# Eight columns of an input projection: high and low weights side by side in one stationary tile

## The chip, the cores and the metric

The kernel runs on one core of one Trainium2 chip. The metric is the device time of one execution in microseconds (us), as the median of several runs. A profile shows one execution of the same program, with every instruction of the five engines: TensorE (PE, with its weight loads as PEld), VectorE (DVE), ScalarE (ACT), GpSimd (POOL) and SyncE (SP), whose queue issues nearly all DMAs here. Each engine takes its instructions in the order in which the program has them. An instruction that waits holds up all that stand behind it on its engine.

## The reference

One layer of a hybrid decoder (2048 tokens, width 1024): one input projection feeds four gated DeltaNet heads and four HGRN2 heads, then an output projection, an MLP and a gated embedding follow. Cut to what the change touches:

```python
proj = jnp.einsum('btd,dc->btc', hn, w_in[i]).astype(f32)
...
a_gdn = proj[..., OFF_GDN_A:OFF_GDN_B]      # 4 columns
b_gdn = proj[..., OFF_GDN_B:OFF_HG_F]       # 4 columns
...
beta = jax.nn.sigmoid(b_gdn)
g_dec = -jnp.exp(gdn_a_log[i].astype(f32)) * jax.nn.softplus(a_gdn + gdn_dt_bias[i].astype(f32))
o_a = gated_delta_rule_chunked(q_a, k_a, v_a, g_dec, beta)
```

`a_gdn` gives each DeltaNet head its decay, `b_gdn` its gate. These eight columns of the input projection are what the change is about.

## The kernel before

**Precision.** All large products are made to nearly float32 accuracy out of a faster format (`F32R`). A float32 operand is split into a high part (a rounded copy, made by ScalarE) and a low part (what is left, a subtraction on VectorE); `split` at L164 and L165 does this. A product then takes three passes over the stationary operand: high weights by high data, high weights by low data, low weights by high data.

**Tiling of the mixer stage.** The 2048 tokens go in four quarters `q` of 512. For each quarter 33 *works* are run one after another on TensorE. The first is `ab`: the eight columns, spread in a stationary tile of 128 columns so that the four decays come out on partitions 0 to 3 of the result and the four gates on partitions 32 to 35; the other columns are zero. Then come eight works for each of four heads, of 128 columns each: k, q, v and z of the DeltaNet head, then f, i, q and g of the HGRN2 head. A work is 8 blocks of 128 input rows by 3 passes, 24 matmuls of 128x128 by 128x512, all into one bank of PSUM (`mm_...`, L1072). This document counts the four `ab` works as blocks 0 to 3, by their quarter.

**Weights.** In the first quarter the weights of a work are loaded raw and split (`stage`, L484), and both halves are written to a cache in device memory (`keep`, L180). In the later quarters they are loaded back already split (`reload`, L185), one MB a work. Three such tiles exist at a time.

**The order around the works.** TensorE's and SyncE's orders are written by hand. Each work is cut into three *steps* of eight matmuls. After each step, and once in its middle, the clock of the kernel moves and the generators due then issue their next portion: their matmuls are put between those of the works. The DeltaNet mixers (`gdn_mixer`), the HGRN2 mixers (`hgrn_mixer`) and the decays' own post-processing (`decays`) are such generators, with their due steps in tables (`A_STEPS`, `B_STEPS`). VectorE's, ScalarE's and GpSimd's orders are chosen by a scheduler when the program is built, so an edit at one place can move other instructions on these engines.

**What runs at an `ab` block.** At blocks 1 to 3 the heads of the quarter before are still under way:

- head 2's DeltaNet recurrence, a chain from chunk to chunk: `psa` on PE (L764), `r` on DVE (L766), `psb` on PE (L769), `w` on ACT (L771), `psc` on PE (L774), the new state `S` on DVE (L776), and `psa` of the next chunk. Two of its chunks lie around the block.
- head 3's triangular solve on DVE (`pr`, `xs`: L698, L701, L703), whose result goes through device memory (`xd`, L708; `xt`, L715), is transposed on DVE (`xn`, L717) and used on PE (`psp`, L722). The next head's solve starts with copies into `pr` and `xs` (L693, L695).
- the HGRN2 heads: `qk_h`, `att_h` and `keys_h` (L820 to L860), and the closing norms of finished heads (`og`, `osq`, `hl`, `m`; `nrm` on PE, L270 and L271).
- the next quarter's data: scaling and splitting of `xt` on DVE and ACT.

**The decays.** `decays` takes the result of the block from PSUM. ScalarE adds the bias to the four decay rows (`sp`, L498) and takes the tanh of the four gate rows (`gb`, L500). Softplus follows as |sp| on DVE (`se`, L502), Exp and Ln on ACT (L503, L504, each with a load of ScalarE's tables), then two operations on DVE (L505, L506) and four running sums (L508). The sums go to device memory (`gd`, L512) and, transposed by PE (`ps_gb`, L519), into `gcol` (L522).

```python
            S.activation(sp, ps[0:4, :], AF.Identity, bias=dec[:, 1:2])
            V.memset(gb, 0.0)
            S.activation(gb[32:36, :], ps[32:36, :], AF.Tanh, scale=0.5)
```

## Time and profile before

| what | value |
|---|---|
| median of 3 runs | 2715.93 us (2712.65 to 2716.56) |
| span of the profiled execution | 2719.9 us |
| mean granted TensorE clock | 0.995 |
| matmuls on PE | 12745, of them 96 in the four `ab` blocks |
| start of the four `ab` blocks | 40.2, 285.5, about 544.1 and 805.4 us |
| mixer stage | about 40 to 1065 us |

The profile's page gives the busy time of each engine over the whole span; a timeline lists instructions in order of time, neighbours of one line merged. A row of the timeline has the start in us, the duration in us, the engine, the line and operation, what is written and read, the number of instructions merged, and in brackets, where the engine stood idle before it, for how long and what ended the wait. Durations of neighbours overlap a little: the next instruction starts before the last has written its end. A table by windows gives, for stretches of time, the busy time of each engine with the number of its instructions, the granted clock, the busy share of the DMA engines and the GB/s that they moved.

### The profile page before, as it was taken

What the parts mean: (1) busy time and instruction counts of PE and PEld (TensorE: products, weight loads), DVE (VectorE), ACT (ScalarE), POOL (GpSimd) and SP (SyncE); (2) the same over time, 40 slices, a digit from 0 to 9 for tenths busy, and PEclk for the clock granted to TensorE, in tenths of its full rate; (3) what the DMA queues carried; (4) which work ended last, traced back from release to release, by engine and by line L of the source; (5) the groups of instructions that cost most, each with busy time, mean ns of one, the idle gap of its engine ahead of it and who ended that gap; (6) DMA issues with size and microseconds to landing.
All of it is one profiled execution on the core that took longest, in us unless ns stands there. A gap on an engine that the chain in (4) does not pass through costs nothing.

```text
span 2719.9 us, 38475 instructions
## 1 busy us (share of the span) xinstructions
PE 2660.8 (98%) x12745; PEld 2215.1 (81%) x12745; DVE 2040.8 (75%) x4219; ACT 1464.0 (54%) x2940; POOL 118.5 (4%) x133
## 2 busy tenths in 40 slices
PE   8999999999999999998999999999999999999999
PEld 6788888888888887876788888888888888888887
DVE  7778878787777777576989867768787765567776
ACT  7665555465445455575655646555555545465432
POOL 0000000000000000011000000001000000001000
PEclk9999999999999999998999999999999999999999
DMA  8777777667666665887566457667454346577663
GB/s 282 273 237 255 236 263 242 216 214 241 213 201 221 223 213 164 271 281 231 177 232 228 175 178 240 216 202 244 164 196 163 139 172 207 193 256 247 216 212 131
DMA packets 268742, 589.24 MB, mean 217 GB/s; under 512 B 55658, under 2 KB 60232, under 8 KB 249344
## 3 DMA queue, kind: packets, MB, share of 16 engines
q1 hardware_dynamic: 266240, 582.59, 63.9%
q0 software_dynamic: 2304, 4.20, 0.9%
q8 instruction: 101, 1.65, 0.3%
q14 instruction: 97, 0.79, 0.1%
HBM read 419.75 MB, written 166.92 MB: 216 GB/s over the span
## 4 chain that ended last, share of the span: by engine, by line
PE 51%; DMA 3%; DVE 3%; issue 3%; ACT 1%; POOL 1%; SPq 0%; POOLq 0%; DVEq 0%; ACTq 0%
PE d L1143 22%; PE u L1143 22%; PE mmg L1143 6%; PE mmo L1143 1%; DMA raw_out<-in_w_out_dram 1%; DMA yo<-in_xT_dram 0%; PE mme L191 0%; POOL acc_y L234 0%; DMA b<-h1d 0%; DMA w_out<-cache_out 0%; DMA db<-hid 0%; DVE t L165 0%; DMA h1d<-yo 0%; POOL yo L1229 0%; DVE pr_g L698 0%
## 5 line engine op out<-in xcount | busy, mean ns | idle before, releaser
L1072 PE MATMUL mm<-xt,w 128*128 128x512 f32 x3072 | 784.1, 400 | 1.4 <-ACT zt_zg L577 1.1
L1072 PEld LDWEIGHTS mm<-xt,w 128*128 128x128 f32 x3072 | 553.3, 189 | 102.3 <-ACT zt_zg L577 1.5
L1143 PE MATMUL d<-db,da 128*128 128x512 f32 x2688 | 611.0, 389 | 0.5 <-ACT db L217 0.2
L1143 PE MATMUL u<-t,wu 128*128 128x512 f32 x2604 | 591.1, 389 | 0.0
L1143 PEld LDWEIGHTS d<-db,da 128*128 128x128 f32 x2688 | 504.3, 188 | 106.4 <-DVE db L218 1.0
L1143 PEld LDWEIGHTS u<-t,wu 128*128 128x128 f32 x2604 | 488.7, 188 | 101.5
L218 DVE TENSOR_TENSOR db<-db 128x512 fp32r<-128x512 f32 x224 | 159.9, 714 | 72.4 <-ACT db L217 71.7
L1495 DVE TENSOR_TENSOR u<-u,u 128x512 f32<-128x512 f32 x224 | 150.2, 681 | 58.1 <-PE u L1143 56.6
L1143 PE MATMUL mmo<-mixT,w_out 128*128 128x512 f32 x720 | 173.4, 402 | 11.8 <-DMA w_out<-cache_out 5.5
L217 ACT ACTIVATE db<-db 128x512 fp32r<-128x512 f32 x224 | 140.9, 629 | 78.2 <-DMA db<-hid 71.9
L1143 PEld LDWEIGHTS mmo<-mixT,w_out 128*128 128x128 f32 x720 | 139.5, 195 | 44.6 <-DMA w_out<-cache_out 5.9
L1143 PE MATMUL mmg<-h2T,wg 128*128 128x512 f32 (+1 forms) x792 | 174.8, 383 | 0.0
L1538 ACT ACTIVATE u<-u 128x512 f32<-128x512 f32 x128 | 80.8, 631 | 166.3 <-DVE u L1495 166.0
L1143 PEld LDWEIGHTS mmg<-h2T,wg 128*128 128x128 f32 x792 | 145.5, 188 | 29.1
L165 DVE TENSOR_TENSOR da<-da 128x512 fp32r<-128x512 f32 x128 | 93.7, 732 | 77.7 <-ACT da L164 77.1
L164 ACT ACTIVATE da<-da 128x512 fp32r<-128x512 f32 x128 | 80.5, 629 | 124.8 <-DMA da<-sumd 91.6
L164 ACT ACTIVATE wu<-a 128x512 fp32r<-128x512 f32 x124 | 75.0, 623 | 44.3 <-DMA a<-in_w_up_dram 43.0
L698 DVE TENSOR_TENSOR pr_g<-xs_g,sys_g 128x16 f32<-128x16 f32 (+14 forms) x240 | 94.4, 393 | 5.6
L165 DVE TENSOR_TENSOR wu<-a,wu 128x512 fp32r<-128x512 f32 x124 | 85.6, 693 | 10.8 <-ACT wu L164 10.5
L234 POOL TENSOR_TENSOR acc_y<-acc_y,sq_y 128x512 f32<-128x512 f32 x28 | 38.5, 1374 | 1261.6 <-ACT sq_y L233 1260.8
L1539 ACT ACTIVATE u<-u 128x512 f32<-128x512 f32 x128 | 80.5, 629 | 3.1
L165 DVE TENSOR_TENSOR da<-dr,da 128x512 fp32r<-128x512 f32 x96 | 66.3, 691 | 19.0 <-ACT da L164 16.5
(385 smaller groups left out, 3792.6 us busy)
## 6 DMA issues: line engine op xcount, KB each, us to landing
w<-cache_in SPq DMA_DIRECT2D x96, 1024.0 KB
db<-hid SPq DMA_DIRECT2D x224, 256.0 KB
cache_in<-w SPq DMA_DIRECT2D x32, 1024.0 KB
hid<-u SPq DMA_DIRECT2D x128, 256.0 KB
da<-sumd SPq DMA_DIRECT2D x128, 256.0 KB
a<-in_w_up_dram SPq DMA_DIRECT2D x124, 256.0 KB
hid<-ht SPq DMA_DIRECT2D x96, 256.0 KB
dr<-in_w_down_dram SPq DMA_DIRECT2D x96, 256.0 KB
```

What stands on the lines that cost most here:

```text
L164: S.activation(t[:, 0], raw, AF.Copy)
L165: eng.tensor_tensor(t[:, 1], raw, t[:, 0], ALU.subtract)
L217: S.activation(t[:, 0], plain(t), AF.Copy)
L218: V.tensor_tensor(t[:, 1], plain(t), t[:, 0], ALU.subtract)
L234: eng.tensor_tensor(acc, acc, sq, ALU.add)
L698: V.tensor_tensor(pr[:, :, :, 0:i], xs[:, None, :, 0:i].broadcast_to([P, 2, GC, i]), sys[:, 0:i, i : i + 2].rearrange("p j two -> p two j" ...
L1072: PE.matmul(ps, *terms[i], start=i == 0, stop=i == nt - 1)
L1143: PE.matmul(ps, a, b, start=start, stop=stop)
L1495: V.tensor_tensor(c[new], c[old], ps, ALU.add)
L1538: S.activation(c[k], c[k], AF.Relu)
L1539: S.activation(c[k], c[k], AF.Square)
```

## The change

For the `ab` work alone, the high weights of the eight columns are put into columns 0 to 63 of the stationary tile and the low weights into columns 64 to 127. One pass then makes the products of both with the same data. Per block of input rows two passes remain (all weights by high data, all weights by low data), 16 matmuls a work in place of 24; the low-by-low product comes with it. High and low results stand on partitions 0 to 35 and 64 to 99 of the bank and are added afterwards: ScalarE copies the lower 36 rows to SBUF, VectorE adds the upper 36 rows from PSUM, and what read PSUM before reads this sum.

- The raw load takes half the columns (128x8x64, rows of 256 bytes), the split works on half, the cache and its three reloads hold 512 KB in place of 1024 KB.
- The three steps of the work have 5, 5 and 6 matmuls in place of 8 each, and the generators' portions lie at the same steps.

```diff
+        def stage_ab():
+
+            raw = wp.tile([P, KD, P // 2], F32, tag="raw", name="raw_ab0", bufs=2)
+            nc.sync.dma_start(raw, w_ab[:, :, : P // 2])
+
+            def ready():
+                w = wp.tile([P, KD, P], F32R, tag="whl", name="w_ab0")
+                S.activation(w[:, :, : P // 2], raw, AF.Copy)
+                V.tensor_tensor(w[:, :, P // 2 :], raw, w[:, :, : P // 2], ALU.subtract)
+                return w
...
         def decays(ps, q):
 
             gb = mt(f"gb_{q}", "gb", 1, (36, QT))
-            sp = m2.tile([4, QT], F32, tag="tmp", name=f"sp_{q}")
+            rest = m2.tile([36, QT], F32, tag="th", name=f"ab_rest_{q}")
+            ab = m2.tile([36, QT], F32, tag="tmp", name=f"ab_{q}")
             se = m2.tile([4, QT], F32, tag="th", name=f"se_{q}")
-            S.activation(sp, ps[0:4, :], AF.Identity, bias=dec[:, 1:2])
+            S.activation(rest, ps[P // 2 : P // 2 + 36, :], AF.Copy)
+            V.tensor_tensor(ab, ps[:36, :], rest, ALU.add)
+            sp = ab[0:4, :]
+            S.activation(sp, sp, AF.Identity, bias=dec[:, 1:2])
             V.memset(gb, 0.0)
-            S.activation(gb[32:36, :], ps[32:36, :], AF.Tanh, scale=0.5)
+            S.activation(gb[32:36, :], ab[32:36, :], AF.Tanh, scale=0.5)
...
                 for k, xk in enumerate(xt):
+                    if h is None:
+                        terms += [(w[:, k, :], xk[:, 0, :]), (w[:, k, :], xk[:, 1, :])]
+                        continue
                     terms += [(w[:, 0, k, :], xk[:, 0, :]), (w[:, 0, k, :], xk[:, 1, :]), (w[:, 1, k, :], xk[:, 0, :])]
```

`keep_ab` and `reload_ab` do for this tile what `keep` and `reload` do for the others. In the built programs PE and SP have the same order as before but for the changed instructions. On VectorE and ScalarE the scheduler has moved others around blocks 0 to 3. For blocks 2 and 3 the order on VectorE after the chunk's state `S` is:

```
before: ... xs_g, r_g, xs_g, se, gb, pr_g, xs_g copy, m_h, sp, att_h, sp, att_h, scans x4, qk_h, xn_g, copy_predicated, S_g, og_g, osq_g, gbb
after:  ... r_g, xs_g, add(ab), xs_g, gg_h, pr_g, xs_g, se, xs_g, gb, pr_g copy, att_h, att_h, qk_h, sp, m_h, copy_predicated, sp, S_g, scans x4, og_g, osq_g, xn_g, gbb
```

(`sp` stands for the two operations of L505 and L506, which after the change work on the tile `ab`.) In block 1 `xn_g` stands behind the scans too, ahead of `og_g`, and `m_h` stands between the two `att_h`. On ScalarE the order before is bias, tanh, table load, Exp, `w_g`, table load, Ln; after the change it is copy, bias, tanh, `w_g`, table load, Exp, table load, Ln.

More of the change, by code (lines that the diff above doesn't have):

```diff
@@ L491, in stage, with keep_ab, reload_ab @@
             return ready
+        def stage_ab():
[6 more added lines that the diff above has]
+                return w
+            return ready
+        def keep_ab(w):
+            cached["ab"] = dr.tile([P, KD * P], F32, name="cache_ab")
+            nc.sync.dma_start(cached["ab"], w.bitcast(F32).rearrange("p k n -> p (k n)"))
+        def reload_ab(q):
+            w = wp.tile([P, KD, P], F32R, tag="whl", name=f"w_ab{q}")
+            nc.sync.dma_start(w.bitcast(F32).rearrange("p k n -> p (k n)"), cached["ab"])
+            return w
         def decays(ps, q):
             gb = mt(f"gb_{q}", "gb", 1, (36, QT))
-            sp = m2.tile([4, QT], F32, tag="tmp", name=f"sp_{q}")
+            rest = m2.tile([36, QT], F32, tag="th", name=f"ab_rest_{q}")
+            ab = m2.tile([36, QT], F32, tag="tmp", name=f"ab_{q}")
             se = m2.tile([4, QT], F32, tag="th", name=f"se_{q}")
-            S.activation(sp, ps[0:4, :], AF.Identity, bias=dec[:, 1:2])
+            S.activation(rest, ps[P // 2 : P // 2 + 36, :], AF.Copy)
+            V.tensor_tensor(ab, ps[:36, :], rest, ALU.add)
+            sp = ab[0:4, :]
+            S.activation(sp, sp, AF.Identity, bias=dec[:, 1:2])
             V.memset(gb, 0.0)
-            S.activation(gb[32:36, :], ps[32:36, :], AF.Tanh, scale=0.5)
+            S.activation(gb[32:36, :], ab[32:36, :], AF.Tanh, scale=0.5)
             V.tensor_scalar(gb[32:36, :], gb[32:36, :], 0.5, 0.5, ALU.mult, ALU.add)
@@ L971, in stage_work @@
             if j < len(works) and works[j][3] == 0:
-                staged[j] = stage(works[j][0], works[j][2])
+                staged[j] = stage_ab() if works[j][4] is None else stage(works[j][0], works[j][2])
         def split_work(j):
             if j < len(works):
-                split_w[j] = staged.pop(j)() if j in staged else reload(works[j][1], works[j][0])
+                if j in staged:
+                    split_w[j] = staged.pop(j)()
+                elif works[j][4] is None:
+                    split_w[j] = reload_ab(works[j][3])
+                else:
+                    split_w[j] = reload(works[j][1], works[j][0])
         def keep_work(j):
             if works[j][3] == 0:
-                keep(works[j][1], split_w[j])
+                if works[j][4] is None:
+                    keep_ab(split_w[j])
+                else:
+                    keep(works[j][1], split_w[j])
         def load_x(q):
```

## The prediction

> **What bounds the kernel now.** I read the page first, then tables by windows around the `ab` blocks, then the timelines there. The page has PE busy for 98% of the span, and the window from 560 to 820 us (one quarter, with its `ab` block) says it again, at full clock.

> ```profile
> 560.00:820.00 260.00, 253.97 (x1393) 215.20 (x1391) 198.21 (x580) 136.80 (x362) 13.83 (x17) 1.00 0.68 222
> 541.00:548.00 7.00, 7.00 (x39) 5.94 (x38) 7.00 (x19) 4.14 (x9) 0.00 (x0) 1.00 0.63 238
> 548.00:555.00 7.00, 6.52 (x32) 5.10 (x32) 6.89 (x22) 2.88 (x4) 0.00 (x0) 1.00 0.04 17
> ```

> The columns are the window, its length, the busy us of PE, PEld, DVE, ACT and POOL, then clock, DMA share and GB/s. The last two rows lie on block 2. Over the quarter VectorE has a quarter of its time free; here it has none: 7.00 of 7.00 us, then 6.89. So at the place of the change two engines bind, and the question is which of them a shorter block leaves as the bound.

> The timeline of block 2, and under it the same place of block 3:

> ```profile
> 551.12 0.36 DVE L776 SCALAR_TENSOR_TENSOR S_g<-S_g,cd_g,psc_g 128x128 f32<-128x128 f32 x1
> ...
> 551.54 0.49 PE L764 MATMUL psa_g<-S_g,y_kg 128*128 128x128 f32 x2 [0.48 <-DVE S_g L776]
> ...
> 812.89 0.49 PE L764 MATMUL psa_g<-S_g,y_kg 128*128 128x128 f32 x2 [0.46 <-DVE S_g L776]
> ```

> PE is through with the block at 551.06 and waits 0.48 us for `S_g`, which DVE only reaches at 551.12, in a queue without a gap. `psc_g`, which `S_g` needs, stands in PE's order ahead of the block's last 12 matmuls, so `S_g` is late for DVE's queue, not for its input. In block 1 PE and `S_g` arrive together, with no wait.

> **What is removed: 32 matmuls.** Block 0 runs its 24 without a gap:

> ```profile
> 40.22 5.73 PE L1072 MATMUL mm_ab<-xt,w_ab 128*128 128x512 f32 x24 [0.21 <-ACT sq_e L233]
> ```

> 5.73 / 24 = 0.24 us each, a little less without the last one's own end; I take 0.23. Eight fewer a block are 1.85 us, four blocks 7.4 us.

> **Where this goes, blocks 1 to 3.** PE comes to `psa_g` 1.85 us earlier. On DVE nothing up to `S_g` is changed or moved, and none of it waits for the `ab` matmuls, so `S_g` ends where it did and `psa_g` starts where it did. The wait grows from 0.48 to about 2.3 us (block 3 the same, block 1 from nothing to 1.9). Gain 0 in each. If DVE did come earlier by the whole 1.85 us, it would be 5.6 us over the three; I take 0, since the queue shows no gap.

> **What is added, and who is late.** A copy of 36x512 on ACT and an addition of 36x512 on DVE with one operand in PSUM, both at the head of the decays' chain. The rows of the chain in block 2, first ACT's, then DVE's, then the row of PE that waits for them:

> ```profile
> 550.98 0.43 ACT L826 ACTIVATE hb_h<-qk_h 128x256 f32<-128x256 f32 x1 [3.60 <-DVE qk_h L824]
> 551.31 0.67 ACT L498 ACTIVATE sp<-mm_ab,dec 4x512 f32<-4x512 f32 x1
> 552.00 0.59 ACT L500 ACTIVATE gb<-mm_ab 4x512 f32<-4x512 f32 x1
> 552.61 1.28 ACT L503 ACT_TABLE_LOAD   x1
> 555.24 0.63 ACT L503 ACTIVATE se<-se 4x512 f32<-4x512 f32 x1 [1.35 <-DVE se L502]
> 555.90 0.37 ACT L771 ACTIVATE w_g<-psb_g,cc_g 128x128 f32<-128x128 f32 x1
> 556.28 1.28 ACT L504 ACT_TABLE_LOAD   x1
> 557.58 0.63 ACT L504 ACTIVATE se<-se 4x512 f32<-4x512 f32 x1
> ```

> ```profile
> 558.24 0.68 DVE L505 SCALAR_TENSOR_TENSOR sp<-sp,se 4x512 f32<-4x512 f32 x1 [1.32 <-ACT se L504]
> 558.85 0.41 DVE L842 TENSOR_TENSOR att_h<-at_h_d,cst 128x256 f32<-128x256 f32 x1
> 559.19 0.47 DVE L506 TENSOR_SCALAR sp<-sp,nexpa 4x512 f32<-4x512 f32 x1
> 559.58 0.40 DVE L844 TENSOR_TENSOR att_h<-at_h,cst 128x256 f32<-128x256 f32 x1
> 559.91 1.35 DVE L508 TENSOR_TENSOR_SCAN gb<-one,sp 4x128 f32<-4x128 f32 x4
> 561.19 0.39 DVE L855 TENSOR_TENSOR qk_h<-qk_h,gg_h 128x256 f32<-128x256 f32 x1
> 561.51 0.42 DVE L717 STREAM_TRANSPOSE xn_g<-xt_g 128x256 f32<-128x256 f32 x1
> 561.87 0.68 DVE L860 COPY_PREDICATED att_h<-cst,at_h 128x256 f32<-128x256 uint32 x1
> 562.37 0.29 DVE L776 SCALAR_TENSOR_TENSOR S_g<-S_g,cd_g,psc_g 128x128 f32<-128x128 f32 x1
> 562.60 0.66 DVE L585 TENSOR_TENSOR og_g<-pso_g,zt_zg 128x512 f32<-128x512 f32 x1
> 563.20 0.66 DVE L587 TENSOR_TENSOR osq_g<-osq_g,q_g 128x512 f32<-128x512 f32 x1
> ```

> ```profile
> 561.99 0.71 PE L722 MATMUL psp_g<-xn_g,um 128*128 128x128 f32 x4 [0.38 <-DVE xn_g L717]
> ```

> DVE itself stands idle here, 1.32 us at 558.24, for the Ln. So the chain to the Ln sets DVE's time, and DVE's `xn_g` sets PE's at `psp_g`.

> The two new operations have no row of their own. The nearest are `gb` for the copy (512 columns from PSUM, 0.59) and `og_g` for the addition (512 columns, one operand in PSUM, 0.66). Rows of 4 and of 128 partitions take alike (L505 0.68, L585 0.66), so the 36 partitions do not matter. Bounds 0.5 to 0.8 each; I take 0.59 and 0.66. With the new orders:

> - ACT, copy: `hb_h` ahead of it is held by DVE until 550.98, so it starts at 551.31, where `sp` did, and ends at 551.9.
> - DVE, addition: it stands behind `r_g` and one reduction, so that its turn comes at about 552.9 (by the distances of starts around there); to 553.6.
> - ACT: bias to 554.3, tanh to 554.9, `w_g` (now ahead of the loads) to 555.3, table load to 556.6, Exp to 557.2, table load to 558.5, Ln to 559.15. Before, it ended at 558.21: 0.94 later. `w_g` comes earlier than it did, so `psc_g` on PE does not wait.
> - DVE from the Ln on, by the distance of starts (a little under the durations): `sp` 0.6, `m_h` 0.1, the predicated copy 0.5, the second `sp` 0.4, `S_g` 0.25, the scans 1.28, then `og_g` and `osq_g` 0.6 each, which now stand ahead of `xn_g`. The two `att_h` and `qk_h` have gone into the idle time before. 559.2 + 4.3 = 563.5, and `xn_g` ends at 563.95 where it ended at 561.93.

> So `psp_g` starts 2.0 us later. About 0.2 of it comes back at PE's next wait for DVE (`nrm_g`, quoted below for block 1), for `hl_g` is then early. Blocks 2 and 3, which have the same orders: +1.8 us each.

> Block 1 has a bigger wait at `psp_g` already:

> ```profile
> 299.85 0.17 DVE L695 COPY xs_g<-cst 128x8 f32<-128x8 f32 x1 [3.85 <-DMA xd_g<-xs_g]
> ...
> 301.30 0.15 DVE L280 TENSOR_SCALAR m_h<-m_h 128x4 f32<-128x4 f32 x1
> ...
> 303.91 0.71 PE L722 MATMUL psp_g<-xn_g,um 128*128 128x128 f32 x4 [1.35 <-DVE xn_g L717]
> ...
> 307.29 0.50 PE L271 MATMUL nrm_g<-hl_g,ones 128*128 128x512 f32 x1 [0.17 <-DVE hl_g L165]
> ```

> DVE is held until 299.85 by a transfer, and this covers the longer chain: by the same steps the Ln ends at 300.5, when DVE is at `att_h`. But `m_h` now stands between the two `att_h`, and its own transfer lands by 301.3 at the latest; I take 301.1. Behind it `att_h` 0.35, `qk_h` 0.33, `sp`, the copy, `sp`, `S_g` and the scans as above make 3.7, to 304.9, and `xn_g` ends at 305.35 instead of 303.86: +1.5, less 0.2 at `nrm_g`, is +1.3 us.

> **Block 0.** PE can end 1.85 us sooner, but the third work of the quarter needs the PSUM bank that DVE's convolution of the first work reads until 58 us:

> ```profile
> 46.07 1.06 ACT L164 ACTIVATE w<-raw 128x1024 fp32r<-128x1024 f32 x1 [1.90 <-DMA raw<-in_w_in_dram]
> ...
> 58.09 2.09 PE L1072 MATMUL mm<-xt,w 128*128 128x512 f32 x8 [0.35 <-DVE acc_kg L542]
> ```

> ACT waits until 46.07 for a transfer, and copy and addition lie under that wait; the rest of the chain starts where it did. I take 0, between -1.85 (the convolution moves up too) and +1.3 (copy and addition both count).

> The halves saved in the cache and in the first split bring nothing: in no row does PE or DVE wait for `w_ab` at blocks 1 to 3. [...]

> **Sum.** 0 + 1.3 + 1.8 + 1.8 = +4.9 us on the profiled 2719.9, 0.18%. The profile is 0.15% above the median, so the step carries over as it is, if the stages behind the mixers follow PE, as I assume: 2715.93 + 4.9 = 2720.8 us.

> **Rivals.**

> - *PE is the bound, and the whole 7.4 us comes off:* 2708.5 us. For it speaks PE's 98%; against it DVE's 7.00 of 7.00 us and the 0.48 and 0.46 us that PE already waits at the block's end. It needs slack in DVE that the rows do not have. 0.12. [...] The rows have a second full engine here.
> - *The saving dies at `S_g`, but the longer chain is hidden:* 2715.9, give or take 2.5. The 1.32 us that DVE idles before the Ln, and other matmuls that DVE holds up behind, would have to take it up. 0.23.
> - *Slower by more:* in the work after next PE waits for ACT's `y_qg`:

> ```profile
> 582.28 0.49 PE L659 MATMUL kk_g<-y_qg,y_kg 128*128 128x128 f32 x2 [1.05 <-ACT y_qg L551]
> ```

>   In the changed order a table load ahead of it stands behind a read of PE's `t_kg`. If ACT's whole load of 1.28 us comes on top in each of three quarters, it is 2720.8 + 3.8 = 2724.6. It decides if ACT has no slack left there. 0.25.
> - *My forecast:* 2720.8, its own range 2717.5 to 2723. 0.40.

> **Chances.** A measurement of this kernel can tell about 0.2%, 5.4 us, from no change: faster is below 2710.5, slower above 2721.4. The first rival and a tail of the second make faster 0.14. The third and 0.17 of my own case lie above: 0.42. The rest, 0.44, is within. The range, 2712 to 2725.5, takes in the second and third and leaves out the first.

> **What would show it.** Right: `psa_g` waits about 2 us for `S_g` at blocks 1 to 3; `psp_g` waits some 2.4 us for `xn_g` in blocks 2 and 3; the distance from `S_g` to the end of the Ln grows by about 1 us; PE's busy time falls by about 7 us and the span does not follow. Wrong: `S_g` comes earlier after the block's start than it did (the first rival), or `xn_g` is as early as before (the second), or `kk_g` waits over 2 us for `y_qg` (the third).

## The result, and the profile after

| | before | after |
|---|---|---|
| median of 8 runs each, side by side | 2716.18 us (2711.54 to 2719.97) | 2724.45 us (2719.33 to 2730.66) |
| ratio to before, 95% interval | 1 | 1.0037 (1.0026 to 1.0047) |
| span of the profiled execution | 2719.9 us | 2724.6 us |
| PE busy, matmul instructions | 2660.8 us, 12745 | 2653.8 us, 12713 |

The change makes the kernel slower: by 8.3 us between the medians, 10 us by the ratio (7 to 13 by its interval). The forecast was +4.9 us, and the likeliest of its three outcomes was no change clear of noise (0.44), ahead of slower (0.42). The time lies inside its range, near the upper end, but only because the range takes in the third rival, whose cause did not come (see below).

The three windows that opened the prediction, in the profile after (window, length, busy us of PE, PEld, DVE, ACT and POOL, granted clock, DMA share, GB/s):

```profile
560.00:820.00 260.00, 252.38 (x1373) 215.13 (x1372) 198.82 (x582) 135.15 (x361) 14.75 (x17) 0.99 0.66 221
541.00:548.00 7.00, 6.91 (x36) 5.55 (x36) 7.00 (x20) 4.80 (x10) 0.00 (x0) 1.00 0.44 164
548.00:555.00 7.00, 5.09 (x22) 3.91 (x22) 6.99 (x21) 1.76 (x3) 0.00 (x0) 0.88 0.13 54
```

DVE is as full as it was (6.99 of 7.00 us), and PE is busy for 1.4 us less in the last window. New is the last row's clock: 0.88 where it was 1.00. The timeline of block 2 after, PE's rows and those that they wait for:

```profile
551.77 0.34 DVE L803 SCALAR_TENSOR_TENSOR S_g<-S_g,cd_g,psc_g 128x128 f32<-128x128 f32 x1
...
552.16 0.49 PE L791 MATMUL psa_g<-S_g,y_kg 128*128 128x128 f32 x2 [1.91 <-DVE S_g L803]
...
552.40 4.58 PE L1110 MATMUL mm<-xt,w 128*128 128x512 f32 x12
...
560.87 0.63 ACT L531 ACTIVATE se<-se 4x512 f32<-4x512 f32 x1
561.53 0.68 DVE L532 SCALAR_TENSOR_TENSOR ab<-ab,se 4x512 f32<-4x512 f32 x1 [1.27 <-ACT se L531]
...
565.82 0.42 DVE L744 STREAM_TRANSPOSE xn_g<-xt_g 128x256 f32<-128x256 f32 x1
...
566.30 0.71 PE L749 MATMUL psp_g<-xn_g,um 128*128 128x128 f32 x4 [2.51 <-DVE xn_g L744]
...
567.49 3.40 PE L1110 MATMUL mm<-xt,w 128*128 128x512 f32 x8
...
586.33 0.38 PE L685 MATMUL kk_g<-y_kg 128*128 128x128 f32 x2
587.71 0.49 PE L686 MATMUL kk_g<-y_qg,y_kg 128*128 128x128 f32 x2 [0.99 <-ACT y_qg L578]
```

Both forecast waits are there: 1.91 us for `S_g`, 2.51 us for `xn_g`. And `psa_g` starts where it did: 7.44 us behind the start of its block (552.16 - 544.72), before 7.49 (551.54 - 544.05). But the 12 matmuls behind the first wait take 4.58 us, and the 8 behind the second 3.40 us. The same two groups before, and the start of `kk_g`, which is used below:

```profile
551.78 2.98 PE L1072 MATMUL mm<-xt,w 128*128 128x512 f32 x12
...
562.90 2.09 PE L1072 MATMUL mm<-xt,w 128*128 128x512 f32 x8
...
580.85 0.38 PE L658 MATMUL kk_g<-y_kg 128*128 128x128 f32 x2
```

After the change again, the same stretch in windows of 3.4 us, laid on the places where the trace's clock records change:

```profile
546.50:549.90 3.40, 3.40 (x20) 2.88 (x18) 3.40 (x10) 0.59 (x1) 0.00 (x0) 1.00 0.68 285
549.90:553.30 3.40, 1.49 (x8) 1.01 (x7) 3.40 (x12) 1.03 (x2) 0.00 (x0) 0.99 0.00 0
553.30:556.70 3.40, 3.40 (x10) 2.63 (x9) 3.32 (x11) 1.35 (x2) 0.00 (x0) 0.50 0.00 0
556.70:560.10 3.40, 3.40 (x22) 3.00 (x21) 1.17 (x4) 2.81 (x4) 0.00 (x0) 1.00 0.18 34
560.10:563.50 3.40, 3.40 (x20) 2.82 (x18) 2.13 (x7) 2.79 (x6) 1.01 (x1) 1.00 0.83 294
563.50:566.90 3.40, 0.89 (x7) 0.60 (x6) 3.40 (x9) 0.63 (x1) 0.00 (x0) 1.00 0.09 25
566.90:570.30 3.40, 3.40 (x12) 2.82 (x12) 3.17 (x8) 1.28 (x5) 0.00 (x0) 0.50 0.54 142
```

Read PE's busy time (the third number) against the clock of the row below. In the two windows that hold a wait PE is busy for 1.49 and 0.89 us of 3.4; in the window after each the granted clock is 0.50, and then it is whole again. In the profile before, no window between 40 and 1065 us is at half clock. After the change there are five: at 75.4 us (behind block 0), 553.3, 566.9, 816.1 and 829.7.

What this does to PE in block 2, from the first matmul of the block to the first `kk_g`, before and after:

```profile
544.05:580.85 36.80, 35.79 (x190) 29.55 (x188) 31.55 (x85) 22.82 (x58) 3.00 (x4) 1.00 0.62 197
544.72:586.33 41.61, 37.09 (x181) 30.45 (x180) 32.57 (x88) 23.54 (x59) 2.60 (x4) 0.92 0.51 175
```

PE stands idle for 4.5 us where it was 1.0: the 3.5 us more are the two waits, as forecast. But its busy time, which eight matmuls fewer should have brought down by about 1.85 us, went up by 1.3 us. The difference, an estimated 3.15 us, is near the 3.4 us that two windows at half clock can cost at most.

So there were two theories to tell apart. **A:** TensorE's waits lower its clock, and each half-clock window costs up to 1.7 us (half of 3.41 us, the length of one half-clock record in the trace) on top of the wait. **B:** the longer chain of the decays delays enough on ScalarE and VectorE to cost all of it, and the clock only goes along.

### The profile page after: what moved, and what is told of

It is laid out like the page before. It is cut to its first block, busy times and chain, and to the rows that moved or that the text cites. A ratio compares the mean times of both kernels' runs of the same rounds, so it can differ in the third digit from the quotient of the medians.

```text
span 2724.6 us, 38415 instructions
## 1 busy us (share of the span) xinstructions
PE 2653.8 (97%) x12713; PEld 2211.2 (81%) x12713; DVE 2040.6 (75%) x4223; ACT 1465.6 (54%) x2944; POOL 119.5 (4%) x133
## 4 chain that ended last, share of the span: by engine, by line
PE 53%; DMA 4%; DVE 4%; issue 3%; ACT 1%; POOL 1%; SPq 0%; POOLq 0%; DVEq 0%; ACTq 0%
PE u L1181 22%; PE d L1181 21%; PE mmg L1181 6%; PE mm L1110 2%; PE mmo L1181 1%; DMA raw_out<-in_w_out_dram 1%; POOL acc_y L234 1%; DMA yo<-in_xT_dram 0%; DMA b<-h1d 0%; DVE pr_g L725 0%; DMA rd_g<-m_g 0%; DMA w_out<-cache_out 0%; DVE t L165 0%; ACT sq_y L233 0%; PE mme L191 0%
## 5 line engine op out<-in xcount | busy, mean ns | idle before, releaser
L165 DVE TENSOR_TENSOR da<-da 128x512 fp32r<-128x512 f32 x128 | 95.9, 749 | 76.8 <-ACT da L164 76.0
L164 ACT ACTIVATE da<-da 128x512 fp32r<-128x512 f32 x128 | 80.5, 629 | 122.2 <-DMA da<-sumd 99.9
L164 ACT ACTIVATE wu<-a 128x512 fp32r<-128x512 f32 x124 | 75.1, 623 | 47.1 <-DMA a<-in_w_up_dram 45.4
L234 POOL TENSOR_TENSOR acc_y<-acc_y,sq_y 128x512 f32<-128x512 f32 x28 | 38.6, 1380 | 1260.0 <-ACT sq_y L233 1260.0
L165 DVE TENSOR_TENSOR wu<-a,wu 128x512 fp32r<-128x512 f32 x124 | 85.6, 692 | 9.5 <-ACT wu L164 9.0
L165 DVE TENSOR_TENSOR da<-dr,da 128x512 fp32r<-128x512 f32 x96 | 66.3, 690 | 17.3 <-ACT da L164 15.6
```

The lines of the kernel that those rows point to most:

```text
L164: S.activation(t[:, 0], raw, AF.Copy)
L165: eng.tensor_tensor(t[:, 1], raw, t[:, 0], ALU.subtract)
L234: eng.tensor_tensor(acc, acc, sq, ALU.add)
```

## The experiments

One measure serves them all: the stretch from the first matmul of an `ab` block to the first `kk_g` behind it (L658 before, L685 after). In block 2 it is 36.8 us before (580.85 - 544.05) and 41.6 us after (586.33 - 544.72). The spans of single profiles are too coarse for this: two of the kernel before are 2719.9 and 2711.2 us, while their stretches agree within 0.5 us a block. In the table "half clock" lists the starts of the half-clock windows between 40 and 1065 us, and the ratio is to the kernel before in runs on the same chip.

| kernel | blocks 0, 1, 2, 3 (us) | half clock at (us) | ratio (95%) |
|---|---|---|---|
| before | 28.2, 37.3, 36.8, 36.8 | none | 1 |
| before_again | 27.8, 37.7, 36.8, 37.0 | none | one run |
| after | 28.5, 37.9, 41.6, 41.6 | 75, 553, 567, 816, 830 | 1.0037 (1.0026 to 1.0047) |
| after_again | 28.6, 38.0, 40.0, 40.2 | 77, 565, 825 | one run, +6.9 us |
| e1_short_alone | 27.8, 35.8, 38.6, 37.6 | 548 | 0.9996 (0.9986 to 1.0006) |
| e2_long_chain_alone | 29.5, 38.7, 39.5, 39.2 | none | 1.0023 (1.0014 to 1.0032) |
| e3_fill_waits | 27.4, 38.8, 38.9, 38.9 | 75 | 1.0016 (1.0007 to 1.0025) |
| e5_fill_half | 27.3, 38.4, 38.6, 38.4 | 75 | one run, +6.0 us |
| w1_wait_in_before | 27.8, 41.2, 39.7, 38.2 | 306, 566 | one run, +8.7 us |
| e4_defer_softplus | 28.3, 36.7, 39.4, 39.5 | 563, 822 | 1.0021 (1.0013 to 1.0030) |
| p1_hgrn_on_pool | 28.6, 41.3, 41.3, 39.8 | 289 (two windows), 572, 814 | 1.0039 (1.0026 to 1.0051) |
| p2_decays_on_pool | 31.7, 40.3, 43.5, 44.0 | 60, 309, 569 (two), 821, 835 (two) | 1.0061 (1.0047 to 1.0075) |
| p3_both_on_pool_after | 31.9, 44.1, 41.7, 43.2 | 59, 288 (two), 571, 814, 834 | 1.0062 (1.0049 to 1.0074) |
| p3_both_on_pool_before | 30.2, 43.3, 41.3, 41.6 | 290, 311, 553, 833 | 1.0046 (1.0033 to 1.0058) |
| v1_later_after | 28.1, 40.6, 37.0, 38.6 | 76, 308 (two windows), 827 | 1.0004 (0.9995 to 1.0014) |
| v1_later_before | 28.3, 37.6, 37.8, 38.7 | 812 | 1.0010 (1.0002 to 1.0019) |
| v4_later_half | 28.5, 38.5, 39.2, 39.2 | 566, 826 | 1.0010 (1.0001 to 1.0020) |
| v3_later_nrm_after | 28.3, 37.3, 38.4, 36.8 | 76, 568 | 0.9992 (0.9983 to 1.0001) |
| v3_later_nrm_before | 28.4, 37.3, 38.8, 37.2 | 559 | 1.0007 (0.9997 to 1.0016) |
| v5_later_and_defer | 28.6, 36.8, 35.8, 35.6 | none | 0.9976 (0.9966 to 0.9986) |

### The two parts of the change, each alone

`e1_short_alone`: the 16 matmuls with the packed tile, the decays as they were.

```diff
...
-            S.activation(rest, ps[P // 2 : P // 2 + 36, :], AF.Copy)
-            V.tensor_tensor(ab, ps[:36, :], rest, ALU.add)
-            sp = ab[0:4, :]
-            S.activation(sp, sp, AF.Identity, bias=dec[:, 1:2])
+            S.activation(sp, ps[0:4, :], AF.Identity, bias=dec[:, 1:2])
...
```

> Two theories of the 8.3 us that the changed kernel lost (2724.45 against 2716.18). Theory A, the clock: the waits of psa for S_g (1.9 us) and of psp for xn (2.5 us) in blocks 2 and 3 each let TensorE's granted clock fall to half for one 3.4 us stretch, some 1.7 us lost each time, on top of the waits themselves. Theory B, the chain alone: the copy and the addition make the decays late on ScalarE and VectorE, and this costs all of it. Here the block keeps its 16 matmuls, but the decays read rows 0 to 36 of mm_ab directly, with no copy and no addition (the products of the low weights are computed and left out of the result). A: psa still waits about 1.9 us for S_g, so one half-clock stretch stays after it in blocks 2 and 3, psp waits no more than before (about 0.4 to 1 us): 2717 to 2720. B: nothing is late but S_g, whose time does not depend on the change, so the time is that of before or less, 2709 to 2716.

The time is that of before: 2712.51 against 2713.26 us, ratio 0.9996 (0.9986 to 1.0006). 32 matmuls fewer gave nothing that can be measured. That is in the range of Theory B; Theory A had expected 2717 to 2720 with a window lost in both blocks, and one was lost. `psa` waits alike in blocks 2 and 3, yet only one of them lost its clock:

```profile
547.12 0.49 PE L787 MATMUL psa_g<-S_g,y_kg 128*128 128x128 f32 x2 [1.91 <-DVE S_g L799]
...
805.92 0.49 PE L787 MATMUL psa_g<-S_g,y_kg 128*128 128x128 f32 x2 [1.93 <-DVE S_g L799]
```

The first wait lies inside one window (545.0 to 548.4), the second across the border of two (near 804.4). Block 2 took 1.0 us longer than block 3.

But the zero is a sum that cancels. Block 1 gained 1.4 us, since `psp` does not wait there any more. In block 3, with the clock whole, the stretch grew by 0.8 us, and `psp` waits 1.2 us in blocks 2 and 3 where it waited 0.4. The scheduler chose another order on VectorE here too, with `og_g` and `osq_g` ahead of `xn_g`, as in the changed kernel, though no operation was added to the chain:

```profile
558.91 0.67 DVE L610 TENSOR_TENSOR osq_g<-osq_g,q_g 128x512 f32<-128x512 f32 x1
559.51 0.43 DVE L740 STREAM_TRANSPOSE xn_g<-xt_g 128x256 f32<-128x256 f32 x1
...
559.99 0.71 PE L745 MATMUL psp_g<-xn_g,um 128*128 128x128 f32 x4 [1.23 <-DVE xn_g L740]
```

So part of what `xn_g` loses in the changed kernel comes from this order, and the runs do not part the short block from it.

`e2_long_chain_alone`: the copy (partitions 64 to 99 of the bank, by ScalarE) and the addition (partitions 0 to 35 from PSUM, by VectorE) put into the kernel before, which keeps its 24 matmuls.

> The kernel before with its 24 matmuls in the block, and with the copy of rows 64 to 99 and the addition ahead of the decays (those rows are zero here, so the result is the same). B: the chain alone costs what the change cost, 2722 to 2725. A: psa waits 0.5 us as before, psp waits for xn by the added 1 to 2 us; where that wait stays under 1.7 us, the longest wait that left the clock whole in the changed kernel, the clock stays whole and only the wait is paid: 2717 to 2720; where it passes 1.9 us, half-clock stretches come after psp and the time goes to 2721 or more.

The chain alone, with the order that the scheduler makes of it, costs +6.2 us (3.8 to 8.7 by the interval), and no window of the mixer stage is at half clock. The time is in the range of Theory A and below that of Theory B, but the waits are not where either theory put them. In block 2 `psp` waits 0.3 us for `xn`; new are three tiles (`psc`, `psd`, `nrm`) that wait for ScalarE or VectorE (PE's waits, us, times, longest):

```profile
PE psc_g L778 <- ACT w_g L775: 0.8, 1, 0.8
PE psd_g L726 <- ACT part L754: 0.8, 1, 0.8
PE psa_g L768 <- DVE S_g L780: 0.5, 1, 0.5
PE psp_g L726 <- DVE xn_g L721: 0.3, 1, 0.3
PE nrm_g L271 <- DVE hl_g L165: 0.3, 1, 0.3
PE nrm_g L270 <- ACT hl_g L164: 0.3, 1, 0.3
```

### The waits filled

`e3_fill_waits`: the changed kernel with matmuls on data at hand put into PE's waits; the real ones overwrite what they leave. `e5_fill_half` has 3 and 4 in place of 6 and 8.

```diff
+                if h == 2 and c == NC - 1 and q < NQ - 1:
+                    for i in range(6):
+                        xk = xts[q + 1][i]
+                        PE.matmul(full, xk[:, 0, :P], xk[:, 0, :], start=True, stop=True)
                 PE.matmul(psa, kg[:, blk(c)], s, start=True, stop=True)
...
+            if h == 3 and q < NQ - 1:
+                for i in range(8):
...
             pairs(psp, um[5], two(xn))
```

> The changed kernel, and in blocks 1 to 3 six matmuls of 128x512 into psa's own bank just ahead of psa, and eight into psp's bank just ahead of psp; the real matmuls overwrite them. Nothing else is changed, and 42 matmuls (about 10 us of TensorE) are added where TensorE waits. A: TensorE is kept busy through the waits, the granted clock stays whole in blocks 2 and 3, and 4 stretches of 1.7 us come back: 2716 to 2720. B: S_g and xn come when they came, and the time stays at 2724 to 2725; if TensorE's own work were the bound, it would be 2731 to 2735.

> As the run with six and eight matmuls ahead of psa and psp, with three and four: about half of each wait is filled, and waits of about 1.2 us for S_g and 1.6 us for xn are left. If a wait has to pass some 1.7 to 1.9 us to lower the clock, it stays whole in blocks 2 and 3 and the stretch from the block to the next head's kk_g is 39 us, as with the full filling; if the share of idle time in a stretch counts, half-clock stretches stay and it is over 40 us.

42 more matmuls made the kernel faster: from 1.0037 to 1.0016 of before (+4.3 us). Blocks 2 and 3 take 38.9 us where they took 41.6, with the clock whole. The half filling leaves waits of 1.2 and 1.7 us and does the same (38.6 and 38.4 us). Its windows, on its own grid:

```profile
549.40:552.80 3.40, 2.17 (x11) 1.50 (x11) 3.40 (x11) 1.03 (x2) 0.00 (x0) 1.00 0.00 0
552.80:556.20 3.40, 3.40 (x18) 2.85 (x17) 3.28 (x10) 2.86 (x4) 0.00 (x0) 1.00 0.00 0
563.10:566.50 3.40, 2.09 (x13) 1.92 (x14) 3.40 (x8) 1.49 (x5) 0.00 (x0) 1.00 0.85 260
566.50:569.90 3.40, 3.40 (x17) 2.52 (x17) 2.98 (x10) 2.77 (x5) 0.00 (x0) 1.00 0.95 353
```

PE is busy for 2.1 us and more of the two windows that hold a wait, and the next window keeps the clock; in block 3 one window has 1.7 us of work and the next keeps the clock too. So Theory A holds for the windows in blocks 2 and 3, and what is left with the clock whole there, +4.3 us, is the chain and its waits: both theories have a share.

### A wait of that length without the change, and second profiles

`w1_wait_in_before`: the kernel before with `psp` eight matmuls earlier in PE's order, so that PE reaches it 2 us sooner and waits longer for an `xn` that comes when it came.

```diff
+                if q < NQ - 1 and h == 3:
+                    a_steps = tuple(29 if o == 30 else o for o in a_steps)
                 at(t, gdn_mixer(q, h, g), a_steps)
```

> The kernel before, with nothing of the change in it; only psp is issued eight matmuls (2 us) sooner in blocks 1 to 3, so that TensorE waits about 2.4 us for xn in blocks 2 and 3 where it waited 0.4. Theory A: the granted clock falls to half after these waits, as it does after the changed kernel's, and the stretch from the block to the next head's kk_g grows by the wait of 2 us and by 1.7 us of clock, from 36.8 us to some 40.5. If the clock's fall belongs to the packed tile and not to the wait, the clock stays whole and the stretch is at most 38.8 us.

`psp` waits 2.2 us in block 2 and in block 3, by the same instructions. The windows around both, block 2 first:

```profile
562.20:565.60 3.40, 1.41 (x9) 0.90 (x7) 3.40 (x10) 0.77 (x2) 0.00 (x0) 1.00 0.76 275
565.60:569.00 3.40, 3.19 (x10) 2.71 (x11) 3.10 (x8) 2.38 (x8) 0.00 (x0) 0.51 0.78 62
...
821.66:825.07 3.41, 2.21 (x13) 1.61 (x11) 3.01 (x10) 1.23 (x2) 1.01 (x1) 1.00 0.23 48
825.07:828.48 3.41, 2.40 (x13) 2.08 (x14) 3.41 (x9) 2.52 (x8) 0.00 (x0) 1.00 0.97 366
```

In block 2 the wait falls into one window, PE is idle for 2 us of it, and the next window has half the clock. In block 3 the border at 825.07 cuts the wait in two (1.2 and 1.0 us idle) and the clock stays whole. The stretches are 39.7 us (40.5 was expected) and 38.2 us: the half clock costs 1.5 us here. In block 1 `psp` waits 3.8 us, and the window behind is at half clock as well. So neither the packed tile nor the chain is needed for it; a wait of 2 us is enough, and where it lies on the grid decides.

> The changed kernel once more, for a second profile. Theory A takes the fall of the clock to follow from the waits of 1.9 and 2.5 us: the half-clock stretches come again in blocks 2 and 3. If they are gone and the time with them, they were an accident of one profiled execution.

> The kernel before once more, for a second profile: the stretches from the block to kk_g come again at 36.8 us in blocks 2 and 3 with the clock whole, whatever lies between the blocks; if they differ by over 0.5 us from the first profile's, the comparison of stretches is worth less than it looks.

Before repeats: 36.8 and 37.0 us in blocks 2 and 3, clock whole. After repeats in its waits (1.9 and 2.5 us) but not in its windows: this time only those behind `psp` were at half clock, and blocks 2 and 3 took 40.0 and 40.2 us in place of 41.6.

### The decays' chain shortened or moved

`e4_defer_softplus`: the decays go on with the softplus two steps later.

```diff
+            yield
             V.scalar_tensor_tensor(se, sp, -1.0, sp, ALU.mult, ALU.max)
...
-                        at(clock[0], decays(ps, q), (0, 2, 3, 5) if q else (0, 2, 4, 7))
+                        at(clock[0], decays(ps, q), (0, 2, 3, 4, 6) if q else (0, 0, 2, 4, 7))
```

> The changed kernel with the softplus of the decays (from the absolute value on) issued two steps later, and what follows it one step later. On VectorE the transposition that writes xn then stands ahead of the scans, no longer behind them. Both theories expect psp's wait to shrink by the scans' 1.35 us, to about 1.1 us. A: with it the half-clock stretches after psp go in blocks 2 and 3, 1.4 + 1.7 us a block: 2717 to 2720. B: 1.4 us a block in three blocks: 2720 to 2721.

VectorE's wait for the Ln fell from 1.27 to 0.65 us, but in blocks 2 and 3 the scheduler still has the scans ahead of `xn` (only in block 1 they changed places). `psp` waits 2.0 us there and both blocks lose one window. The time, 2719.06 us, lies in the range of Theory A, but not for the reason given: the window behind `psp` is lost, and the one behind `psa` is not, though `psa` waits 1.9 us. The interval of the ratio (1.0013 to 1.0030) overlaps that of after, so a gain is not shown.

`p1_hgrn_on_pool`, `p2_decays_on_pool` and `p3_both_on_pool_...` move work from VectorE to GpSimd (p3 with the packed weights and with the kernel before):

```diff
+            E = G if h == 3 and q < NQ - 1 else V
-            V.tensor_tensor(by_half(own, 1), side(qq, QT, 1, False), side(k, QT, 1, False), ALU.mult)
+            E.tensor_tensor(by_half(own, 1), side(qq, QT, 1, False), side(k, QT, 1, False), ALU.mult)
...
-            V.tensor_tensor(ab, ps[:36, :], rest, ALU.add)
+            S.activation(ab, ps[:36, :], AF.Copy)
+            G.tensor_tensor(ab, ab, rest, ALU.add)
...
-            V.scalar_tensor_tensor(sp, sp, 0.0, se, ALU.max, ALU.add)
-            V.tensor_scalar(sp, sp, nexpa, None, ALU.mult)
+            G.tensor_scalar(sp, sp, 0.0, None, ALU.max)
+            G.tensor_tensor(sp, sp, se, ALU.add)
+            G.tensor_scalar(sp, sp, nexpa, None, ALU.mult)
```

> The changed kernel, with the five multiplications that open hgrn_mixer (the ones at att_h, qk_h, gg_h) put on GpSimd for the heads that run beside blocks 1 to 3, so that about 2.4 us of VectorE work no longer stands ahead of S_g. Theory A (waits plus the clock that falls to half after them): S_g comes 1.5 us sooner, psa waits under 0.5 us and the half-clock stretch after it goes; xn is still set by the decays' chain, so psp waits 2.5 us or more and its half-clock stretch stays: 2718 to 2723 where the changed kernel has 2724.5. Theory B (the chain of the decays costs it all): PE only waits for xn what it no longer waits for S_g, and the time stays at 2723 to 2725.

> The changed kernel, with the decays' addition, maximum, sum and factors on GpSimd (the first half of mm_ab is copied by ScalarE as well); VectorE keeps the absolute value and the scans and no longer waits for the logarithm. psa still waits 1.9 us. Theory A: xn is written about 2 us sooner, psp's wait falls under 1 us and the half-clock stretches after psp go: 2715 to 2720. Theory B: the chain is as long as in the changed kernel or longer, since a GpSimd operation takes 1.4 us where VectorE takes 0.7, and the time stays at 2722 or goes up.

> Both moves to GpSimd together, with the 16 matmuls of the change. Theory A: neither psa nor psp waits over 1 us, the clock stays whole, and the 8 matmuls saved in a block begin to count, 1 to 1.9 us in each of three blocks against before: 2710 to 2715. Theory B: as p2, 2720 or more.

> The same two moves in the kernel before, with its 24 matmuls in a block. What VectorE had in the way is gone here too, so its waits for S_g (0.5 us) and xn (0.4 to 1.4 us) go: 2712 to 2716. If the packed weights are worth anything once VectorE is out of the way, this run is 2 to 6 us slower than the one before it; if not, the two are the same.

None of the four gained anything. p1 (2724.97 us), p2 (2731.92) and p3 after (2731.54) miss the ranges of Theory A and lie in those of Theory B. p3 before (2726.70) misses its range, and it is 4.8 us faster than p3 after where 2 to 6 us slower was forecast if the packed weights were worth something. p2 shows why on VectorE's timeline:

```profile
562.90 0.33 DVE L805 SCALAR_TENSOR_TENSOR S_g<-S_g,cd_g,psc_g 128x128 f32<-128x128 f32 x1
567.10 1.36 DVE L537 TENSOR_TENSOR_SCAN gb<-one,ab 4x128 f32<-4x128 f32 x4 [3.88 <-POOL ab L535]
...
569.77 0.43 DVE L746 STREAM_TRANSPOSE xn_g<-xt_g 128x256 f32<-128x256 f32 x1
```

VectorE's work fell and its wait grew: the scans stand ahead of `xn_g` and now wait 3.88 us for GpSimd, whose operations take 0.7 to 1.6 us each, and `psp` waits 5.2 us. Here it is the length of the chain that makes `xn` late, not VectorE's load. In p1 `psa` no longer waits, but `psb` does, for an `r_g` that the scheduler had put behind other work (its waits in block 2):

```profile
PE psb_g L796 <- DVE r_g L793: 2.8, 1, 2.8
PE psp_g L749 <- DVE xn_g L744: 1.8, 1, 1.8
PE psc_g L801 <- ACT w_g L798: 1.2, 1, 1.2
```

That the length of the chain counts is Theory B's point, and it holds for its part of the loss. But each of these kernels has half-clock windows as well, four to five stretches of them in the mixer stage (three in p1), so their times do not tell the theories apart.

### TensorE's own order: useful work into the waits

`v1_later_after` and `v1_later_before` issue `psa` four and `psp` eight matmuls later; `v4_later_half` has `psp` only four later; `v3_...` is v1 with `nrm_g` eight later; `v5_later_and_defer` is v3 with the deferral of e4. The edit of v3 (v1 and v4 leave 55 as it is, and v4 has 30.5 for 31):

```diff
+                if q < NQ - 1 and h == 3:
+                    a_steps = tuple(31 if o == 30 else o for o in a_steps)
+                if q < NQ - 1 and h == 2:
+                    a_steps = tuple({50: 50.5, 55: 56}.get(o, o) for o in a_steps)
                 at(t, gdn_mixer(q, h, g), a_steps)
```

> The changed kernel, with two matmul groups issued later on TensorE in blocks 1 to 3 and nothing else moved: psa four matmuls later and psp eight matmuls later, so that TensorE has main matmuls to do while VectorE writes S_g and xn. If the loss lies in TensorE's waits at these two places and in the clock that falls after them, both waits fall under 1 us, the clock stays whole in blocks 2 and 3, and the time comes to 2711 to 2718. If the decays' chain delays something else as well (the gates, the next head's operands), TensorE meets a new wait behind them and the time stays at 2720 or more.

> The same two moves in the kernel before. Its waits for S_g and xn are 0.4 to 1.4 us, so there are some 2.5 us in three blocks to be had: 2712 to 2716, which tells how much of the gain of the run before this one belongs to the moves and how much to the packed weights.

> The changed kernel with psa four matmuls later and psp only four matmuls later, ahead of nrm_g: psp waits about 1.5 us for xn in blocks 2 and 3 and 0.7 us in block 1, nrm_g then finds hl_g written. No wait is long enough to lower the clock: 2713 to 2717. If it comes out slower than psp eight matmuls later, what counts is the wait itself.

> The changed kernel with psa four matmuls later, psp eight matmuls later, and in the same blocks nrm_g eight matmuls later, which had become the next to wait (1.2 us for ScalarE's half of hl_g and 0.6 us for VectorE's). If the matmuls saved are worth something once nothing waits, the stretch falls from 37 to 38.6 us to 35 to 36.5 us and the time to 2708 to 2713 where before has 2714.2; if another wait takes its place, it stays at 2713 to 2716.

> The kernel before, with the same three moves on TensorE (psa four matmuls later, psp and nrm_g eight). If the gain of the run with the packed weights came from the moves alone, this one has it too: 2711 to 2713. If it came from the 8 matmuls saved in a block, this one stays at 2714 to 2717.

> The changed kernel with psa, psp and nrm_g later on TensorE, as in the run that moved all three, and with the softplus of the decays deferred as in the run that did that alone, so that xn stands ahead of the scans on VectorE. psp's last wait of 1.7 us in blocks 2 and 3 shrinks by the scans' 1.35 us, under 0.5 us; the clock stays whole there: 2709 to 2712 where before has 2714. If the saved matmuls are worth nothing because another wait takes over, 2712 to 2715.

The first two moves (v1) take the loss back to within the noise (1.0004, 0.9995 to 1.0014). The time is in the range that was forecast, but not all of the mechanism came: behind blocks 1 and 3 the clock still falls in the profiled execution, whose time is 4.8 us above the median of its kernel. The same moves give the kernel before nothing (1.0010): there `r_g` comes to stand later on VectorE, and `psb` waits 1.9 us for it. With `psp` only half as late the wait stays 2.6 us in blocks 2 and 3 and so do the half-clock windows; the expected 1.5 us was wrong, though the time (2716.84) lies in the expected range. Moving `nrm_g` as well brings the packed kernel to 0.9992 and the kernel before to 1.0007, both within the noise of no change. With the deferral on top the packed kernel beats the kernel before: 2705.89 against 2712.07 us, 0.9976 (0.9966 to 0.9986), that is 3.8 to 9.2 us, and more than was expected (2709 to 2712). Its waits in block 2 and its stretch, with that of the second profile of before under it:

```profile
PE psa_g L792 <- DVE S_g L804: 1.0, 1, 1.0
PE psp_g L750 <- DVE xn_g L745: 0.7, 1, 0.7
```

```profile
540.71:576.48 35.77, 33.96 (x181) 28.13 (x180) 32.72 (x91) 23.39 (x60) 2.38 (x3) 1.00 0.57 200
```

```profile
543.66:580.48 36.82, 35.84 (x190) 29.54 (x188) 31.53 (x85) 22.54 (x58) 2.72 (x3) 1.00 0.59 197
```

PE is busy 1.88 us less in the stretch, about the price of the eight matmuls, and 1.05 us of it comes off the time. The four stretches together are 2.6 us shorter than in that profile (136.7 against 139.3); the rest of the 6.2 us lies between the blocks and was not traced to a place. The kernel before was not run with the deferral and the moves together, so how much of v5's gain needs the packed weights is open; with the moves alone the two differ by 0.15% (0.9992 and 1.0007), and their intervals overlap.

## Why the prediction was right and wrong, point by point

- *The saving dies at `S_g`: right.* `psa` waits 1.91 us (block 1: 1.41) where about 2.3 (1.9) was forecast, and starts 7.44 us behind the block's start, before 7.49. In e1 the short block gains nothing over the whole kernel, though single blocks gain and lose there. PE's busy time fell by 7.0 us (7.4 forecast) and the span did not follow; that the two numbers agree is partly luck, for half-clock windows lengthen matmuls (12 took 4.58 us where they took 2.98), and between the second profiles it fell by 3.8 us (2655.7 to 2651.9).
- *The longer chain and the new order make `xn_g` late: right for blocks 2 and 3, and to size where the clock is whole.* The second profile after has the clock whole up to `psp` in block 2, which starts at 544.04 there:

```profile
551.09 0.34 DVE L803 SCALAR_TENSOR_TENSOR S_g<-S_g,cd_g,psc_g 128x128 f32<-128x128 f32 x1
...
558.61 0.63 ACT L531 ACTIVATE se<-se 4x512 f32<-4x512 f32 x1
...
564.05 0.71 PE L749 MATMUL psp_g<-xn_g,um 128*128 128x128 f32 x4 [2.52 <-DVE xn_g L744]
```

  The end of the Ln is 8.15 us behind the start of `S_g` (before 7.09): +1.06, where +0.94 was forecast. `psp` starts 20.01 us behind the block's start, before 17.94: +2.07, where 2.0 was forecast. In block 1, where no window is lost, `psp` starts 19.00 us behind the block's start, before 18.41: +0.6 us, where 1.5 was forecast. In the first profile after, the Ln ends 9.73 us behind `S_g`: +2.64, for `w_g`, which now stands ahead of the Exp and the Ln on ScalarE, waits 1.61 us there for PE's `psb`, which stands behind the matmuls at half clock.
- *The sum of the chain: about right in blocks 2 and 3, too high in block 1.* Forecast 0, 1.3, 1.8, 1.8 us for blocks 0 to 3. The changed kernel itself has +0.6 us in block 1 (37.9 against 37.3), with the clock whole, and in block 2 +1.7 us once the 3.15 us of the half clock (an estimate, see the busy times above) are taken off its +4.8. With waits short enough to keep the clock in blocks 1 to 3, e3 measures -0.7, 1.5, 2.1, 2.1 and e5 -0.9, 1.1, 1.8, 1.6 us against the first profile of before (both carry dummy matmuls, and both lose a window behind block 0). Only e3's four terms add up to about the 4.9 us of the forecast.
- *The step that failed: "the wait grows from 0.48 to about 2.3 us ... Gain 0 in each", and the same for `psp` at "+1.8 us each".* Both leave PE's clock at the 1.00 that the windows before show, without a reason for it. Missing from the sum is one term: when waits left PE idle for 1.9 us or more of one 3.4 us window, the next ran at half clock (34 of 34, last table). It costs 1.6 us a time by the busy time in block 2 (an estimate, 3.15 us for two), 1.6 by block 2 of the two profiles after (41.6 against 40.0), 1.5 by w1, 1.6 by v3 (38.4 against 36.8), 1.0 by e1. Two to four such windows in blocks 2 and 3 are 3 to 6 us, and with the chain's 3.6 (e5) to 5.1 us (e3) this makes 7 to 11; 8.3 was measured between the medians, 10 by the ratio. e2 has 6.2 us for the chain, in an order of its own, so the split between the two is known only roughly.
- *Block 0, "I take 0": not quite.* The stretch grew by 0.3 us only, but PE's wait for `zt_zg` behind it grew from 1.07 to 1.81 us and the window from 75.4 us is at half clock:

```profile
74.85 3.34 PE L1110 MATMUL mm<-xt,w 128*128 128x512 f32 x8 [1.81 <-ACT zt_zg L604]
```

  Block 1 starts 1.25 us later than in the first profile before (0.9 to 1.4 over both profiles of each kernel), about the upper bound of +1.3 that the prediction gave.
- *The rivals.* The first (PE is the bound, 2708.5) fell with e1: eight matmuls fewer a block and no gain. The second (chain hidden, 2715.9) fell with e2: the chain alone, in the order that it brings with it, costs 6.2 us. The third named nearly the right time, 2724.6, by the wrong mechanism: `kk_g` waits 0.99 us for `y_qg`, before 1.05. That the measured time lies in the range is luck to this extent, for the range reaches above 2723 for this rival.

## What to carry to other kernels

In this kernel, with TensorE 97% busy, a wait of TensorE is not priced by its length alone: add up to half a clock window (1.0 to 1.6 us came out here) for every wait that can leave TensorE idle for some 1.9 us of one window, or put other matmuls into it; even useless ones helped here (1.0037 to 1.0016 in e3). Taking work off the engine with the highest busy share gained nothing by itself here (0.9996 in e1), where VectorE had no gap at the place where the work was (7.00 of 7.00 us busy). Look there for the engine that has no gap, and give the freed time other matmuls by moving the waiting ones back in a hand-written order (0.9976 in v5, with the deferral). A chain that stands in an engine's fixed order ahead of someone else's operand can delay that operand: here `psp` waited 2.5 us for `xn_g`, and 5.2 us with the chain's work on GpSimd, which took longer over it (p2). When a scheduler chooses the order, read it again after each edit: here it moved the operand itself.

## What the runs showed of the hardware

Half-clock windows start, in each of the 20 profiled executions, on one grid of 3.413 us that lies differently from execution to execution, and last one or two of its windows (behind the mixer stage up to three). The last four of the five that are listed for the kernel after start 140, 144, 217 and 221 times 3.413 us behind the first. I cut the mixer stage (28 to 1060 us) of all 20 into windows on their own grids and took PE's idle time in each as the window less its matmul records, whose ends are modelled:

| PE idle in a window of 3.41 us | windows | next window at half clock |
|---|---|---|
| under 1.6 us | 5971 | 5 (4 of them in stretches of two) |
| 1.6 to 1.9 us | 20 | 7 |
| 1.9 us and more | 34 | 34 |
